# Pairs of heads on the two halves of the array, and bias rows spread in one pass

## Chip, cores and metric
One Trainium2 chip, one core of it. The metric is the device time of one execution in microseconds; three executions of the kernel before gave 1483.94, 1485.22 and 1486.90, median 1485.22.

## What is computed
The input is x of 256 tokens by 1024 features. Two blocks follow each other. The first has two layers under an adaptive norm (shift, scale and gate come from a condition vector): an mLSTM mixer with a SwiGLU FFN, and an HGRN2 mixer with eight experts of which two are taken for each token. The second block is an attention layer with three gated branches and an FFN. What matters here, cut from the reference (256 tokens):

```python
# mLSTM, 8 heads, q and k of 64, v of 128
d = where(mask, b[..., :, None] - b[..., None, :] + li[..., None, :], NEG)   # b = cumsum(log sigmoid f)
m_t = maximum(inter, max(d, axis=-1))                  # a running maximum along the tokens
s = einsum('bhtd,bhsd->bhts', qc, kc) * exp(d - m_t[..., None])
num = ... + einsum('bhts,bhsv->bhtv', s, vc)           # and den = sum of s; h = num / max(|den|, exp(-m_t))

# block attention (moba), 8 heads of 64: with 256 tokens it is causal softmax attention over one block
# forgetting attention (fox), 8 heads of 64
scores = einsum('bhqd,bhkd->bhqk', qc, k) * scale + cq[..., None] - cum[:, :, None, :]
p = softmax(where(causal, scores, -inf));  y = einsum('bhqk,bhkd->bhqd', p, v)
# memory attention, 4 heads of 128, over 256 memory tokens
merged = sigmoid(a_m) * (y_m @ w_br_moba) + sigmoid(a_f) * (y_f @ w_br_fox) + sigmoid(a_c) * (y_c @ w_br_mem)
x = x + merged @ w_out
```

## The kernel before
The activations live transposed, features on the 128 partitions and 256 tokens along the free dimension, in SBUF for the whole program. Weights are streamed from HBM in tiles of 1 MB. Each tile is cut into two fp32r parts: ACT writes the rounded upper part (`whi`, line 175) and VectorE the rest (`wlo`, line 181). A projection is then three fp32r matmuls per chunk (`mm3`: upper by upper, upper by lower, lower by upper). Products between activations, as scores and values, are plain f32 matmuls through `mm` (line 165); in the trace each of these is two passes of weight load and matmul.

PSUM has two sets of four banks of 512 columns: `acc` for the projections and `ps` for all the rest (`bank()`). The framework orders the instructions of each engine at build time, by the order in which the program emits them and by when it reckons their operands to be ready; on the chip each engine takes its list strictly in order. The four banks of a set go round in the order in which the program asks for them. So what the program emits behind a group of head products (for instance the projections for the sigmoid gates, `gates()`, or the next q, `qk()`) is used by that order to fill TensorE between the products of the heads.

*mLSTM.* After the gates, `mrun` [8, 256] holds the running maximum, one row for each head. For each head, one matmul with a column of the identity, repeated over 128 columns, as weights (8 rows, `ident[:8, h]`) spreads that row over all 128 partitions (two f32 passes of 256 columns). Two VectorE operations and an exponential on ACT make the decay matrix. Later a loop over the eight heads takes the scores (q and k of head h lie on partitions 0 to 63 or 64 to 127 of one chunk, so each product uses half of the rows of the array: one matmul of 256 columns, one of 128 for the causal half), multiplies them by the decay, takes the value products on the whole array, and sums over tokens with one-column products into one bank that is held through the loop.

*Causal heads* (`causal_heads`, from line 1265) runs twice, for the block attention without a bias and for the forgetting attention with one. For each of eight heads: a bank, the two score products (64 rows), with a bias two products that spread row h of `cum` [8, 256] (8 rows, four f32 passes), two bf16 products that add the causal mask; then the maximum on VectorE (line 1283), the exponential on ACT, both for two query halves, the reciprocal (1285) and the scaling on VectorE; a bank and three transposes on TensorE (line 1290), a copy to SBUF (line 1292); then the value products, 64 columns of weights, into the upper or lower half of the partitions of a bank that an even head and the odd head behind it share. Behind the odd head `split` makes two fp32r parts of it for the branch's projection. The scores of a head thus wait for a bank that comes free behind an earlier head's transposes or values.

`attention` calls them in the order: q, k and v of moba; the forget logits, their log sigmoid and the running sum `cum`; causal heads of moba; gates; q, k, v of fox; the branch of moba; causal heads of fox; gates; q of the memory heads; the branch of fox; the memory heads.

Of the kernel before, what the change touches and what calls it, by code (L numbers as in the profile page):

```python
# [11 lines left out]
F32 = mybir.dt.float32  # L12
# [126 lines left out]
class Kernel:  # L139
# [61 lines left out]
    def all_weights(self):  # L201
        """the tiles of weights in the order in which the products take them"""
# [39 lines left out]
    def prepare(self, n):  # L242
        """the next n tiles of weights that will be asked for"""
        while len(self.ready) < n and (self.loaded or self.load()):
            self.ready.append(self.parts(self.loaded.popleft()))
# [8 lines left out]
    @contextmanager  # L254
    def behind(self, *instructions):
        """what is ready early stays behind these in the order of issue"""
        with ExitStack() as es:
            for ins in instructions:
                es.enter_context(self.tc.issue_after(ins))
            yield  # L260
# [34 lines left out]
    def last_tile(self, products, ends):  # L295
        """the products of each chunk of 128 columns, chunks of different banks after one another, and
        what comes then, two chunks later for its second part"""
# [15 lines left out]
    def like(self, hl, act, k):  # L313
        """chunk k of what weights, whole or in two parts, are multiplied with"""
        return [x[:, k, :] for x in act] if len(hl) == 2 else (self.full[:, k, :],)

    def proj_t(self, act, n=512, nk=DC, between=None, ends=None):
        """act @ the next n columns of weights, transposed, 256 columns to a bank [P, 2, S]"""
# [26 lines left out]
    def proj_tok(self, act, between=None):  # L345
        """act @ the next 512 columns of weights, tokens on the partitions: one bank for each 128 tokens"""
# [15 lines left out]
    def rsqrt(self, pool, v, tag):  # L362
        """v ** -0.5: a guess from the bits of v, a step of Newton's and one of third order"""
# [19 lines left out]
    def spread(self, out, col, start):  # L383
        """the values col [P, 1] of 128 tokens along the free dimension of every partition"""
        self.mm(out, col.to_broadcast([P, P]), self.cst("ident"), start)

    def token_sums(self, out, sq, start, by=None):
        """out [P, 2, n]: for each token the sums over the partitions of sq [P, S], times by [P, n]"""
# [4 lines left out]
    def stat_begin(self, tag="ps", second=None, together=6):  # L393
        """sums of the squares of x, with second [P, DC, 2] also of x * w, of columns (1, w ** 2)"""
# [7 lines left out]
    def square(self, chunk, c=0):  # L402
        """the squares of chunk c; what is returned sums them over the partitions, the first ones together"""
# [12 lines left out]
    def stat_end(self):  # L416
        """1 / the root mean square of each token on every partition"""
        return self.stat_spread(self.stat_tokens())

    def stat_tokens(self):  # L420
        """1 / the root mean square of each token [P, 2, 1]; with second [P, 2, 2] there is also that
        of the norm of x * w that comes after: with r ** -2 = mean(x ** 2) + EPS it is
        r * (mean((x * w * r) ** 2) + EPS) ** -0.5 = (mean((x * w) ** 2) + EPS * r ** -2) ** -0.5"""
# [8 lines left out]
    def stat_spread(self, r):  # L432
        """[P, 2, n] by token to [P, n, S] on every partition"""
# [10 lines left out]
    def normed(self, x, r, g, shift=None, hold=3):  # L444
        """x * r * g (+ shift) as the pair of parts that the products take"""
# [16 lines left out]
    def scaled(self, x, g, tiles=None):  # L462
        """x * g as the pair of parts that the products take"""
# [8 lines left out]
    def held_factor(self, ps):  # L472
        """a factor for each token, kept on every partition"""
# [4 lines left out]
    def ada_tile(self, layer, j, tag="raw2"):  # L478
        """256 columns of silu(c) @ ada_w + ada_b into two columns of mod"""
# [12 lines left out]
    def ada_until(self, n):  # L492
        """the first n of 48 times 256 columns are done"""
# [10 lines left out]
    def first_norm(self, x):  # L504
        """the norm of x, chunk by chunk as the columns of mod are done; its statistic is under way"""
# [40 lines left out]
    def resid(self, ps, c, gate):  # L546
        """chunk c of x += gate * ps, and its squares for the next norm"""
# [14 lines left out]
    def ffn(self, act, gate=None, between=None, factor=None):  # L562
        """factor gives a factor [P, S] of act that is still to come"""
# [63 lines left out]
    def setup(self):  # L627
# [11 lines left out]
        self.mod = self.t(self.cp, [P, 96], "mod")  # L639

    def conditions(self, pool):
        """silu(c), the same on every partition"""
# [19 lines left out]
    def small(self, out, hl, act):  # L662
        """a product with a few columns of weights, transposed"""
# [3 lines left out]
    def head_norm(self, pool, banks, heads, dst, scale, gain=None, by=None):  # L667
        """banks: 512 columns by token. Each head of a token over its root mean square, times the gain
        [P, head] and turned by the rotary embedding if there is a gain, goes transposed to
        dst [P, 4, S], times scale (a number or [P, 1]). by [P, 2, 1] is a factor of the tokens still to come"""  # L670
# [93 lines left out]
    def memory_norm(self, pool):  # L764
        """the memory times its gain; the factor of each token is still to come"""
# [12 lines left out]
    def log_sigmoid(self, pool, f, tag):  # L778
        """[8, S] rows"""
# [6 lines left out]
        return out  # L786

# [4 lines left out]
    def mlstm(self, pool, act):  # L792
# [47 lines left out]
        decay = []  # L840
        for h in range(8):
            pm = self.bank()
            self.mm(pm[:, :S], self.cst("ident")[:8, h : h + 1].to_broadcast([8, P]), mrun, True)
# [12 lines left out]
        for h in range(8):  # L856
            c, o = h // 2, (h % 2) * 64
            qh, kh = q[o : o + 64, c, :], k[o : o + 64, c, :]
            ps = self.bank()
            self.mm(ps[:, 0:S], kh[:, 0:P], qh, True)  # L860
            self.mm(ps[:, S : S + P], kh[:, P:S], qh[:, P:S], False)
# [21 lines left out]
        # h = num / den, and h over its root mean square is num / sqrt(mean(num ** 2) + EPS * den ** 2)  # L883
# [22 lines left out]
    def lower_bounds(self):  # L906
        """lb and 1 - lb of the second mixer"""
# [8 lines left out]
    def hgrn(self, pool, act):  # L916
# [39 lines left out]
        def scores(q, k, bc, at, cr):  # L956
            """at[s, h, half, t]: the scores inside each half of the tokens, cr across the halves.
            Level n pairs the tokens of each right block of 2^n with the left block beside it; the
            decay is split at the last token of the left block, so no exponent is above 0."""
# [47 lines left out]
        def outputs(g, at, cr):  # L1007
            """the heads' normed outputs"""
# [137 lines left out]
    def experts(self, pool, xt, pos, mask, gate, late):  # L1146
        """the tokens of each expert at slots pos (0 to 127) pass through it, their results are added to x"""
# [117 lines left out]
    def causal_heads(self, pool, q, k, v, y, bias):  # L1265
        """softmax over the keys up to each token; y gets the heads' outputs, transposed"""
        nc = self.nc
        for h in range(8):
            c, o = h // 2, (h % 2) * 64
            qh, kh = q[o : o + 64, c, :], k[o : o + 64, c, :]  # L1270
            ps = self.bank()
            self.mm(ps[:, 0:P], qh[:, 0:P], kh[:, 0:P], True)
            self.mm(ps[:, P:384], qh[:, P:S], kh, False)
            if bias is not None:
                sel = self.cst("ident")[:8, h : h + 1].to_broadcast([8, P])
                self.mm(ps[:, 0:P], sel, bias[:, 0:P], False)
                self.mm(ps[:, P:384], sel, bias, False)
            self.mm(ps[:, 0:P], self.identb, self.upb, False)
            self.mm(ps[:, S:384], self.identb, self.upb, False)
            nm, sm = (self.t(pool, [P, 2], n, 2) for n in ("nm", "sm"))  # L1280
            e = self.t(pool, [P, 384], "e", 2)
            for j, sl in enumerate((slice(0, P), slice(P, 384))):
                nc.vector.tensor_reduce(nm[:, j : j + 1], ps[:, sl], axis=AX.X, op=ALU.max, negate=True)
# [173 lines left out]
```

## Time and profile before
| | us |
|---|---|
| median of three runs | 1485.22 |
| lowest, highest | 1483.94, 1486.90 |
| the profiled execution: span from first to last instruction | 1481.2 |
| TensorE busy | 1429.3 (96%) |
| VectorE busy | 1123.6 (76%) |
| ACT busy | 838.1 (57%) |
| mean granted TensorE clock | 0.977 of full speed |

The page of the profile gives busy time by engine, a picture of the span in slices, the chain of work that ended last and the costliest groups. In rows of a timeline the first column is the start and the second the length of one row (several instructions of one kind behind one another are one row, xN); matmul ends are modelled, so the step from one start to the next is the better measure of what an operation takes. A bracket names the idle time before a row and the engine that ended it. `64*128 64x256` is a weight tile of 64 rows by 128 columns and a moving operand of 64 rows by 256 columns.

### The profile page before, as it was taken

To read this page: it belongs to the slowest core of one execution; us is meant where nothing else is said; L and a number is where in the kernel's file an instruction comes from. 1 tells how busy PE (TensorE), PEld (TensorE's weight loads), DVE (VectorE), ACT (ScalarE), POOL (GpSimd) and SP (SyncE) were. 2 spreads that over 40 slices of the span, in tenths; PEclk is the share of its full clock that TensorE was granted. 3 is DMA by queue.
4 is the path that set the end of the run, shared out by engine and by line. 5 is a ranking of instruction groups with operands and counts; after the bars stand their busy time and mean duration, and the time that the engine had idled before them with its cause. 6 is when DMAs were issued, how large, how long until landed. Compare 5 with 4: busy or idle time off the path is not lost.

```text
span 1481.2 us, 23294 instructions
## 1 busy us (share of the span) xinstructions
PE 1429.3 (96%) x9380; PEld 1292.7 (87%) x9380; DVE 1123.6 (76%) x1738; ACT 838.1 (57%) x1195; POOL 32.9 (2%) x36
## 2 busy tenths in 40 slices
PE   5999899999999998999999999999999999999998
PEld 4789899999999987888888888888878779999998
DVE  6887798887697786897898888888666566765554
ACT  2644444434775655777777777766545355544432
POOL 1000100001000020000000000000000000100000
PEclk7999999999899998999999999999999999999999
DMA  8975599989453334798998998995435234555542
GB/s 335 339 260 195 178 348 353 343 314 337 150 151 109 115 114 145 252 375 309 320 362 305 345 339 303 355 322 192 143 114 169 88 114 143 164 179 191 179 143 86
DMA packets 149508, 343.51 MB, mean 232 GB/s; under 512 B 5904, under 2 KB 27280, under 8 KB 149136
## 3 DMA queue, kind: packets, MB, share of 16 engines
q1 hardware_dynamic: 148240, 341.00, 66.1%
q8 instruction: 76, 1.25, 0.4%
q10 hardware_dynamic: 1152, 0.94, 0.2%
q14 instruction: 40, 0.33, 0.1%
HBM read 340.86 MB, written 1.05 MB: 231 GB/s over the span
## 4 chain that ended last, share of the span: by engine, by line
PE 58%; ACT 1%; DVE 1%; issue 0%; ACTq 0%
PE acc L165 38%; PE ps L165 18%; PE ps L1203 1%; ACT whi L175 1%; PE ps L1290 1%; PE ps L698 0%; DVE wlo L181 0%; ACT L175 0%; PE ps L1413 0%; DVE yel L178 0%; ACT yeh L175 0%; ACT e L175 0%; ACT sg L175 0%; DVE ss L677 0%; DVE e L185 0%
## 5 line engine op out<-in xcount | busy, mean ns | idle before, releaser
L181 DVE TENSOR_TENSOR wlo<-raw,whi 128x1024 fp32r<-128x1024 f32 (+2 forms) x564 | 646.9, 1182 | 148.2 <-ACT whi L175 147.6
L175 ACT ACTIVATE whi<-raw 128x1024 fp32r<-128x1024 f32 (+2 forms) x564 | 547.8, 1016 | 314.1 <-PE acc L165 164.3
L165 PE MATMUL acc<-act_hi,whi 128*128 128x256 f32 x1344 | 382.0, 285 | 2.6 <-ACT act_hi L175 2.4
L165 PE MATMUL acc<-act_lo,whi 128*128 128x256 f32 x1344 | 381.1, 284 | 0.0
L165 PE MATMUL acc<-act_hi,wlo 128*128 128x256 f32 x1344 | 379.6, 283 | 1.3 <-DVE wlo L181 1.3
L165 PEld LDWEIGHTS acc<-act_hi,whi 128*128 128x128 f32 x1344 | 255.2, 190 | 4.7 <-ACT act_hi L175 3.0
L165 PEld LDWEIGHTS acc<-act_hi,wlo 128*128 128x128 f32 x1344 | 255.5, 190 | 1.8 <-DVE wlo L181 1.5
L165 PEld LDWEIGHTS acc<-act_lo,whi 128*128 128x128 f32 x1344 | 255.8, 190 | 0.7
L165 PE MATMUL acc<-whi,act_hi 128*128 128x512 f32 (+1 forms) x560 | 217.5, 388 | 0.1
L165 PE MATMUL acc<-wlo,act_hi 128*128 128x512 f32 (+1 forms) x560 | 216.7, 387 | 0.0
L165 PE MATMUL acc<-whi,act_lo 128*128 128x512 f32 (+1 forms) x560 | 215.6, 385 | 0.0
L165 PEld LDWEIGHTS acc<-whi,act_hi 128*128 128x128 f32 x560 | 105.9, 189 | 20.3 <-issue 0.9
L165 PEld LDWEIGHTS acc<-wlo,act_hi 128*128 128x128 f32 x560 | 105.8, 189 | 20.2 <-issue 1.2
L165 PEld LDWEIGHTS acc<-whi,act_lo 128*128 128x128 f32 x560 | 105.7, 189 | 18.8 <-issue 0.3
L485 DVE SCALAR_TENSOR_TENSOR raw<-raw,cond 128x1024 f32<-128x1024 f32 x96 | 115.3, 1228 | 6.5 <-DMA raw<-in_ada_w_dram 6.5
L165 PE MATMUL ps<-hh,whi 128*128 128x256 f32 x352 | 99.6, 283 | 1.5 <-DVE x L178 1.5
L165 PE MATMUL ps<-hl,whi 128*128 128x256 f32 x352 | 99.5, 283 | 0.0
L165 PE MATMUL ps<-hh,wlo 128*128 128x256 f32 x352 | 99.4, 283 | 0.0
L165 PE MATMUL ps<-wlo,hth 128*128 128x512 f32 x176 | 69.0, 392 | 0.0
L165 PEld LDWEIGHTS ps<-hh,whi 128*128 128x128 f32 x352 | 67.4, 192 | 1.7 <-DVE x L178 1.7
L165 PE MATMUL ps<-whi,htl 128*128 128x512 f32 x176 | 68.8, 391 | 0.0
L165 PE MATMUL ps<-whi,hth 128*128 128x512 f32 x176 | 67.6, 393 | 0.0
(348 smaller groups left out, 1798.2 us busy)
## 6 DMA issues: line engine op xcount, KB each, us to landing
raw<-in_ada_w_dram SPq DMA_DIRECT2D x48, 1024.0 KB, 6.2
raw<-in_moe_w_down_dram SPq DMA_DIRECT2D x40, 1024.0 KB, 6.0
raw<-in_moe_w_up_dram SPq DMA_DIRECT2D x32, 1024.0 KB, 7.3
raw<-in_moe_w_gate_dram SPq DMA_DIRECT2D x32, 1024.0 KB, 7.1
raw<-in_w_in_dram SPq DMA_DIRECT2D x26, 1024.0 KB, 5.2
raw<-in_h_w_in_dram SPq DMA_DIRECT2D x16, 1024.0 KB, 5.8
raw<-in_m_w_in_dram SPq DMA_DIRECT2D x12, 1024.0 KB, 7.3
raw<-in_moe_w_gate_dram SPq DMA_DIRECT2D x16, 768.0 KB, 5.5
```

The source lines that it names most:

```text
L165: self.nc.tensor.matmul(out, l, r, start=start, stop=True, skip_group_check=True)
L175: return self.nc.scalar.activation(out, in_, f, **k)
L181: return self.nc.vector.tensor_tensor(out, a, b, op=op)
L485: last = self.nc.vector.scalar_tensor_tensor(w[:, i, :], in0=w[:, i, :], scalar=1.0, in1=self.cond, op0=ALU.mult, op1=ALU.mult, accum_out= ...
L1203: nc.tensor.transpose(hps[:, f * P : (f + 1) * P], h[:, f * P : (f + 1) * P], self.cst("ident"))
L1290: nc.tensor.transpose(pt[:, j * P : (j + 1) * P], e[:, j * P : (j + 1) * P], self.cst("ident"))
```

## The change
Three things are altered; in the rest of the diff comments and docstrings go.

1. Rows are spread by a product of 128 rows. `two_rows` makes a zeroed [128, 256] fp32r tile with the rounded rows in partitions 0 to 7 and what the rounding left in partitions 32 to 39. `row` multiplies it in one fp32r pass by a column of `pick`, which has ones at h and at 32 + h. `mrun` and `cum` both go this way; the tile of `cum` is made before the causal heads of moba.
2. In the mLSTM the score products of heads h and h + 1 are emitted together for even h, into two banks, in turn on rows 0 to 63 and 64 to 127.
3. `causal_heads` loops over four pairs: the score products of both heads in turn, the bias rows of both, the masks of both; the softmax, transposes and copy of each; then one bank and the value products of both in turn on the two column halves, and `split`. The buffers for e, p, the maxima and sums stay two each.

```diff
+        self.pick = self.t(self.cp, [P, 8], "pick", 1, F32R)
+        nc.vector.tensor_tensor(self.pick, self.cst("ident")[:, 0:8], self.cst("ident")[:, 32:40], op=ALU.add)
...
+    def two_rows(self, pool, rows, tag):
+        both = self.t(pool, [P, S], tag, 1, F32R)
+        self.nc.gpsimd.memset(both.bitcast(F32), 0.0)
+        self.act(both[0:8, :], rows, AF.Copy)
+        self.tt(both[32:40, :], rows, both[0:8, :].bitcast(F32), ALU.subtract)
+        return both
+
+    def row(self, out, both, h, start):
+        self.mm(out, self.pick[:, h : h + 1].to_broadcast([P, P]), both, start)
...
+        mrows = self.two_rows(pool, mrun, "mrows")
         for h in range(8):
             pm = self.bank()
-            self.mm(pm[:, :S], self.cst("ident")[:8, h : h + 1].to_broadcast([8, P]), mrun, True)
+            self.row(pm[:, :S], mrows, h, True)
...
         for h in range(8):
-            c, o = h // 2, (h % 2) * 64
-            qh, kh = q[o : o + 64, c, :], k[o : o + 64, c, :]
-            ps = self.bank()
-            self.mm(ps[:, 0:S], kh[:, 0:P], qh, True)
-            self.mm(ps[:, S : S + P], kh[:, P:S], qh[:, P:S], False)
+            c = h // 2
+            if h % 2 == 0:
+                pair = [self.bank() for _ in range(2)]
+                halves = [(ps, q[o : o + 64, c, :], k[o : o + 64, c, :]) for ps, o in zip(pair, (0, 64))]
+                for ps, qh, kh in halves:
+                    self.mm(ps[:, 0:S], kh[:, 0:P], qh, True)
+                for ps, qh, kh in halves:
+                    self.mm(ps[:, S : S + P], kh[:, P:S], qh[:, P:S], False)
+            ps = pair[h % 2]
...
+        queries = (slice(0, P), slice(P, 384))
+        for c in range(4):
+            pair = [(self.bank(), q[o : o + 64, c, :], k[o : o + 64, c, :]) for o in (0, 64)]
+            for ps, qh, kh in pair:
+                self.mm(ps[:, 0:P], qh[:, 0:P], kh[:, 0:P], True)
+            for ps, qh, kh in pair:
+                self.mm(ps[:, P:384], qh[:, P:S], kh, False)
             if bias is not None:
...
+                for i, (ps, qh, kh) in enumerate(pair):
+                    self.row(ps[:, 0:P], bias[:, 0:P], 2 * c + i, False)
+                    self.row(ps[:, P:384], bias, 2 * c + i, False)
+            for ps, qh, kh in pair:
+                self.mm(ps[:, 0:P], self.identb, self.upb, False)
+                self.mm(ps[:, S:384], self.identb, self.upb, False)
+            probs = []
+            for ps, qh, kh in pair:
...
+                probs.append(p)
+            po = self.bank()
+            heads = [(po[i * 64 : i * 64 + 64], v[:, :, (2 * c + i) * 64 : (2 * c + i + 1) * 64], p) for i, p in enumerate(probs)]
+            for out, vh, p in heads:
+                self.mm(out[:, :S], vh[:, 0, :], p[:, :S], True)
+            for out, vh, p in heads:
+                self.mm(out[:, P:S], vh[:, 1, :], p[:, S:384], False)
+            self.split(y[0][:, c, :], y[1][:, c, :], po[:, :S])
...
+            cum = self.two_rows(pool, cum, "cumrows")
             sa = gates(self.causal_heads(pool, q, k, v, y, None))
```

## Rows read from the trace of the kernel before

**Rows 1.** The page: busy time of each engine, and the chain that ended last.
```profile
PE 1429.3 (96%) x9380; PEld 1292.7 (87%) x9380; DVE 1123.6 (76%) x1738; ACT 838.1 (57%) x1195; POOL 32.9 (2%) x36
...
PE 58%; ACT 1%; DVE 1%; issue 0%; ACTq 0%
```

**Rows 2.** Stretches, mLSTM rows: us, busy of each engine, PE clock, DMA share, GB/s.
```profile
62.00:71.80 9.80, 9.62 (x38) 5.73 (x36) 9.01 (x25) 6.63 (x11) 0.00 (x0) 1.00 0.96 347
71.80:78.60 6.80, 6.80 (x15) 4.51 (x15) 5.32 (x12) 4.66 (x8) 0.00 (x0) 0.50 0.42 135
```

**Rows 3.** Stretches, causal heads of moba and of fox, same columns.
```profile
1054.00:1112.00 58.00, 56.79 (x342) 44.39 (x342) 38.84 (x89) 28.69 (x59) 0.00 (x0) 1.00 0.34 112
...
1140.00:1206.00 66.00, 63.37 (x395) 49.72 (x394) 37.31 (x83) 27.04 (x55) 0.00 (x0) 0.99 0.33 108
```

**Rows 4.** Timeline of TensorE, one fox head and the next: start, us, operation.
```profile
1140.03 0.92 PE L165 MATMUL ps<-k,q 64*128 64x128 f32 x4
1140.88 0.92 PE L165 MATMUL ps<-cum,cst_base 8*128 8x128 f32 x4
1141.73 0.29 PE L165 MATMUL ps<-upb,identb 128*128 128x128 bf16 x2
...
1147.35 0.28 PE L165 MATMUL acc<-act_lo,whi 128*128 128x256 f32 x1
1147.47 0.28 PE L165 MATMUL acc<-act_hi,wlo 128*128 128x256 f32 x1
1147.68 0.86 PE L165 MATMUL ps<-p,raw 128*64 128x256 f32 x4
1148.48 0.92 PE L165 MATMUL ps<-k,q 64*128 64x128 f32 x4
```

**Rows 5.** Timeline of TensorE, mLSTM heads.
```profile
100.53 0.81 PE L165 MATMUL ps<-p,v 128*128 128x256 f32 x4
101.18 0.73 PE L165 MATMUL ps<-cst_base,p 128*128 128x1 f32 x6
101.84 0.70 PE L165 MATMUL ps<-q,k 64*128 64x256 f32 x2
102.46 0.61 PE L165 MATMUL ps<-cst_base,sq 128*128 128x1 f32 x4
103.00 0.49 PE L165 MATMUL ps<-q,k 64*128 64x128 f32 x2
103.41 0.38 PE L165 MATMUL acc<-act_hi,whi 128*128 128x256 f32 x1
```

**Rows 6.** Timeline of TensorE, fp32r passes of 128 columns.
```profile
692.05 0.64 PE L165 MATMUL ps<-identr,disp 128*128 128x128 f32 x4
692.53 0.34 PE L165 MATMUL ps<-disp,xth 128*128 128x256 f32 x1
```

**Rows 7.** Timeline of TensorE, rows of mrun: three heads together, one alone.
```profile
64.31 1.56 PE L165 MATMUL ps<-mrun,cst_base 8*128 8x256 f32 x6
65.70 0.23 PE L837 MATMUL ps<-cst_base,floor 8*128 8x8 f32 x2
...
67.23 0.69 PE L165 MATMUL ps<-mrun,cst_base 8*128 8x256 f32 x2
67.85 0.50 PE L165 MATMUL acc<-whi,act_lo 128*128 128x512 f32 x1
```

**Rows 8.** Timeline of TensorE, the last fox head: masks, transposes.
```profile
1198.40 0.29 PE L165 MATMUL ps<-upb,identb 128*128 128x128 bf16 x2
...
1203.48 0.61 PE L1290 MATMUL ps<-cst_base,e 128*128 128x128 f32 x3 [1.65 <-DVE e L185]
```

**Rows 9.** Stretch behind the last fox head, columns as in rows 2.
```profile
1205.00:1208.40 3.40, 2.93 (x13) 2.32 (x12) 2.65 (x7) 2.06 (x5) 0.00 (x0) 0.50 0.00 0
```

**Rows 10.** Operations on tile mrun: duration ns min/median/max, starts, shapes.
```profile
L181 DVE TENSOR_TENSOR floor<-bsum,mrun x1: 401/401/401, 64.5 to 64.5; 8x256 f32<-8x256 f32 x1
```

**Rows 11.** Timeline of TensorE, first moba head's transpose.
```profile
1062.63 0.30 PE L1290 MATMUL ps<-cst_base,e 128*128 128x128 f32 x1 [1.01 <-DVE e L185]
```

More of the change, by code (lines that the diff above doesn't have):

```diff
@@ L1267, in causal_heads @@
         nc = self.nc
[L1268 to L1273, printed above, removed]
-            if bias is not None:
[L1275 to L1283, printed above, removed]
-                last = self.act(e[:, sl], ps[:, sl], AF.Exp, bias=nm[:, j : j + 1], accum_out=sm[:, j : j + 1])
-            nc.vector.reciprocal(sm, sm)
-            for j, sl in enumerate((slice(0, P), slice(P, 384))):
-                self.ts(e[:, sl], e[:, sl], sm[:, j : j + 1], ALU.mult)
-            pt = self.bank()
-            for j in range(3):
-                nc.tensor.transpose(pt[:, j * P : (j + 1) * P], e[:, j * P : (j + 1) * P], self.cst("ident"))
-            p = self.t(pool, [P, 384], "p", 2)
-            nc.vector.tensor_copy(p, pt[:, :384])
-            if h % 2 == 0:
-                po = self.bank()
-            vh = v[:, :, h * 64 : (h + 1) * 64]
-            self.mm(po[o : o + 64, :S], vh[:, 0, :], p[:, :S], True)
-            self.mm(po[o : o + 64, P:S], vh[:, 1, :], p[:, S:384], False)
-            if h % 2:
-                self.split(y[0][:, c, :], y[1][:, c, :], po[:, :S])
@@ new lines, in causal_heads @@
+        queries = (slice(0, P), slice(P, 384))
[5 more added lines that the diff above has]
+                self.mm(ps[:, P:384], qh[:, P:S], kh, False)
+            if bias is not None:
+                for i, (ps, qh, kh) in enumerate(pair):
[6 more added lines that the diff above has]
+            for ps, qh, kh in pair:
+                nm, sm = (self.t(pool, [P, 2], n, 2) for n in ("nm", "sm"))
+                e = self.t(pool, [P, 384], "e", 2)
+                for j, sl in enumerate(queries):
+                    nc.vector.tensor_reduce(nm[:, j : j + 1], ps[:, sl], axis=AX.X, op=ALU.max, negate=True)
+                    last = self.act(e[:, sl], ps[:, sl], AF.Exp, bias=nm[:, j : j + 1], accum_out=sm[:, j : j + 1])
+                nc.vector.reciprocal(sm, sm)
+                for j, sl in enumerate(queries):
+                    self.ts(e[:, sl], e[:, sl], sm[:, j : j + 1], ALU.mult)
+                pt = self.bank()
+                for j in range(3):
+                    nc.tensor.transpose(pt[:, j * P : (j + 1) * P], e[:, j * P : (j + 1) * P], self.cst("ident"))
+                p = self.t(pool, [P, 384], "p", 2)
+                nc.vector.tensor_copy(p, pt[:, :384])
+                probs.append(p)
[6 more added lines that the diff above has]
+            self.split(y[0][:, c, :], y[1][:, c, :], po[:, :S])
```

## The prediction

> **What bounds the kernel now.** I read the page's busy shares and its chain of waits first. TensorE is busy 96% of the span, and nearly all of the chain that the page gives to an engine is TensorE, with ACT and VectorE at 1% each [rows 1]. So a microsecond of TensorE time taken away should come off the end, and a microsecond in which TensorE stands, in its order, behind an operand goes on. Next I looked at the table of stretches for the stages that the diff touches. In the mLSTM's rows stage (62 to 71.8) TensorE is busy 9.62 of 9.80 us and VectorE 9.01; the stage behind it runs at a granted clock of 0.50, the lower level of 1.2 GHz, for 6.8 us [rows 2]. In the two stages of causal heads TensorE is busy 56.79 of 58 and 63.37 of 66 us, VectorE 38.84 and 37.31, ACT less [rows 3]. Last I read the timeline of TensorE, where the distance from one row's start to the next is what an operation costs in the queue; the durations themselves overlap.
>
> **The sum, part by part.** It is made against the profiled execution: span 1481.2 us. The median of the runs is 1485.2, so 4.0 us lie around the span, and I keep them.
>
> (a) *Bias rows of the Fox heads.* Before, each head has four f32 passes with 8 rows of weights, 0.85 us from start to start (1140.88 to 1141.73) [rows 4]. After, it has two fp32r passes, one of 128 and one of 256 columns. The first size costs 0.12 (four from 692.05 to 692.53) [rows 6], the second 0.12 too (1147.35 to 1147.47) [rows 4]; together 0.24, and I take 0.26. Eight heads: 8 x (0.85 - 0.26) = **-4.7**. Bounds: 0.24 to 0.48 a head, -4.9 to -3.0.
>
> (b) *Fewer switches between whole and half array.* A score group (4 passes, 768 columns) takes 0.85 and a value group 0.80 (1147.68 to 1148.48), with 0.09 more for entering (0.21 instead of 0.12 in front of it, 1147.47 to 1147.68) [rows 4]. Four passes of the same columns on all 128 rows, without a switch, take 0.65 (100.53 to 101.18) [rows 5]. A pair of heads therefore costs 2 x 0.85 + 2 x 0.80 + about 3 x 0.09 = 3.57 us where streaming alone is 2.60; 0.97 is switching, in four places. After the change there are two such places in a pair, so half goes: 0.485 x 8 pairs = **-3.9**. Bounds: -2 (if the groups' own fill is in the 0.97) to -5.
>
> (c) *The two halves at once.* No row of before has products of different halves behind one another, so this is bounded from both sides. Nothing: the passes follow each other as now. All: passes of 0.108 (128 columns) and 0.217 (256), which is 0.65 over 768 columns [rows 5], in the new order A,A,B,B | A,A,B,B, where only neighbours of different halves overlap: 0.108 + 0.108 + 0.217 + 0.217 + 0.217 = 0.87 instead of 1.30. That saves 0.43 in each of 16 groups (scores and values of 8 pairs), 6.9 us. I take **-5.0**, nearer to the upper end: consecutive passes already overlap in the array in these rows (0.28 long at 0.12 spacing) [rows 4], so the engine does not finish one before it starts the next. A loss I exclude: the same passes with the same columns are issued. The Trainium skill, page TensorEngine Tiling (Array Packing), section Key Properties, says that different tiles can load weights and multiply in parallel, and that a change of the tiling mode drains the engine. The second half agrees with the 0.85 against 0.65; the first no row here shows. By the page alone (c) would be -6.9 and (d) 0.8 more, and the time 1460.1, an estimate from that page.
>
> (d) *mLSTM scores.* A head's two products cost 0.62 (101.84 to 102.46) and 0.41 (103.00 to 103.41) with about 0.10 for entering: 1.13 [rows 5], 2.26 a pair. Two groups at 0.65 and one entry and exit (0.28) are 1.58. Four pairs: -2.7. At once would give up to 4 x 0.43 = 1.7 more; I take half, 0.9, because the token sums hold one of the four banks and the second head's scores must wait for a bank to come free. **-3.6**, bounds -2 to -4.4. TensorE has whole-array products of gates and values beside it (100 us and after).
>
> (e) *mLSTM rows.* Three heads behind one another take 1.39 (64.31 to 65.70), a lone one 0.62 (67.23 to 67.85) [rows 7]: 1.39 + 5 x 0.62 = 4.5; after, 8 x 0.12 = 1.0. **-3.5**, bounds -2.5 (VectorE, 92% busy there, is late with the decay) to -4.6 (the entries go too).
>
> (f) *The half-clock stretch behind them.* 6.8 us at 0.50 cost 3.4 us over full clock [rows 2]. What the engine did before it fell was the alternation of 8-row passes with whole ones; the half-clock stretch of [rows 9] follows waits and no such rows, so I take half: **-1.7**, bounds 0 and -3.4.
>
> (g) *The end of the Fox stage.* TensorE is not busy for 2.63 us of the stage [rows 3], mostly in front of the last head's transposes (1.65 us on VectorE) [rows 8], and then runs 3.4 us at half clock, busy 2.93 of them [rows 9], so another 1.5. The cause is eight softmaxes in series: one takes 5.0 us from the masks (1198.40) to the first transpose (1203.48) [rows 8], the scores of a head come only after the values of the one before. Pairs put two chains beside each other, so that the four pairs end sooner than TensorE's work. **-3.0**, bounds 0 and -4.1.
>
> (h) *Costs.* The two parts of the rows are an ACT copy and a VectorE subtraction on 8 x 256, about 0.4 us each (the row nearest to it is 401 ns) [rows 10], and a POOL clearing. Those of Fox are made ahead of the causal heads of the first branch, 80 us before use: nothing. Those of the mLSTM delay its rows by 0.8, behind projections that TensorE has anyway, with more than 15 us until the first decay is used: nothing, and 0.8 without that cover. The selector is one small VectorE operation at the start: nothing. The new order makes new waits: the next pair's scores need banks that come free with the transposes and values of this one, and behind transposes in TensorE's order stand projections that need nothing. One such wait of 1.01 us stands in the first branch before (1062.63) [rows 11]. I take three of them, at the first and last pairs: **+3.0**, bounds 0 and 8.
>
> Sum: -4.7 - 3.9 - 5.0 - 3.6 - 3.5 - 1.7 - 3.0 + 3.0 = **-22.4**. Span 1458.8, time 1462.8: I say **1463**.
>
> **Rivals.** *Halves not at once.* The two halves share what streams; then (c) and the 0.9 of (d) are gone: -16.5, time **1468.7**. For it: no row shows such overlap, and f32 passes come in twos of the same half. Against: the overlap of neighbours in the array.
>
> *The saved time in the attention becomes waiting.* Then scores, masks and values are quick but the softmaxes, on VectorE and ACT, are the length of a stage; (a), (b), (c), (g) are lost, 16.6: -5.8, time **1479.4**. For it: the waits at 1203 and 1062. Against: VectorE is busy only 37.31 of 66 us [rows 3], and two chains beside each other have more slack than one. The Trainium skill, same page, section PSUM Bottleneck, has this as a rule: tiling speeds up TensorE but not what empties PSUM. The busy shares here do not bear it out for a whole stage.
>
> *Slower: TensorE stands at every pair.* The projections that fill a softmax are put in TensorE's order at build time. If they are spent ahead of the first pairs, TensorE stands for most of one chain, say 3.5 of the 5.0 us [rows 8], at each of 8 pairs: 28 us instead of the 3.0 of (h), and (g) isn't saved: -22.4 + 25 + 3.0 = +5.6, time **1490.8**. It decides from 2.8 us a pair on. For it: after the change both heads' values of a pair wait for both softmaxes, and no scores of another pair stand between. Against: the fill of a stage, 63.4 busy less 8 heads of about 3.0 (0.85 + 0.85 + 0.80 and masks, transposes and entries) or some 39 us, is about as long as four chains of pairs.
>
> *The change doesn't do what it says*, for example the scheduler takes the products of a pair apart again: then (a) and (e) alone remain, -8.2, time 1477.0.
>
> **How the numbers follow.** Forecast 0.45, halves not at once 0.30, waiting 0.12, slower 0.08, taken apart 0.05. The forecast's own range, with the bounds of (c), (f), (g) and (h), is 1453 to 1468. Ranges of the first rival, 1465 to 1473, and some of the waiting case put the range that should hold 8 in 10 at **1453 to 1480**. About 0.2%, 3 us, is what a measurement can tell from no change: faster takes the forecast, the first rival, most of the waiting case and the last, 0.85; same some of the waiting case and of the slower one, 0.07; slower 0.08.
>
> **What would show it.** Fox scores of a pair at about 0.9 to 1.1 us from the first product to the first row product is (c); 1.3 or more is the first rival. Rows of a head at 0.25 is (a). The stretch at about 72 at a clock of 1.00 is (f); the Fox stage without idle time in front of the last transposes is (g). If TensorE's idle time in front of transposes and values in the two stages sums to more than 8 us, (h) is wrong, and above 22 the kernel is slower. The prediction is wrong if the granted clock falls in the new pair groups, or if a stretch outside these stages moves by more than 2 us.

## The result, and the profile after

| | before | after |
|---|---|---|
| median, first measurement (4 runs each) | 1484.58 | 1466.79 (1455.06 to 1472.68) |
| median, second measurement (15 and 6 runs) | 1484.13 | 1466.96 (1462.43 to 1471.64) |
| ratio, with its 95% interval | | 0.9873 [0.9842, 0.9903], then 0.9881 [0.9859, 0.9903] |
| profiled execution: span, mean granted clock | 1481.2, 0.977 | 1470.9, 0.969 |

The kernel is 17 to 18 us faster; 22 were forecast, and the time lies inside the stated range. Single runs of one kernel differ by up to 18 us here, so from now on a term is read from a trace wherever a trace can show it, and the times, by median and ratio, are the check on it.

**The pairs.** The timeline of TensorE in the changed kernel, a Fox pair's scores, rows and masks (start, length, operation):

```profile
1143.90 0.28 PE L165 MATMUL acc<-yh,wlo 128*128 128x256 f32 x1
1144.11 0.93 PE L165 MATMUL ps<-k,q 64*128 64x128 f32 x8
1144.96 0.72 PE L165 MATMUL ps<-cumrows,pick 128*128 128x128 f32 x4
1145.53 0.40 PE L165 MATMUL ps<-upb,identb 128*128 128x128 bf16 x4
...
1152.04 1.22 PE L165 MATMUL ps<-p,raw 128*64 128x256 f32 x8
1153.20 0.93 PE L165 MATMUL ps<-k,q 64*128 64x128 f32 x8
```

Eight score passes, two heads, go in 0.85 us (1144.11 to 1144.96), as long as four took for one head [rows 4]; in the single records the passes of the two halves start 7 ns apart. The rows of both heads take 0.57 instead of 2 x 0.85. The values of both take 1.16 instead of 2 x 0.80: they too run side by side, but the second head's start 0.36 later, right when its copy of p ends. VectorE's timeline of the same kernel shows the two copies in one row, so that the second ends at 1152.35; the second head's first pass starts at 1152.40:

```profile
1151.22 1.13 DVE L1315 COPY p<-ps 128x384 f32<-128x384 f32 x2 [0.48 <-PE ps L1313]
```

**The waits.** Of TensorE's timeline in the changed kernel, three places at which it stands (the last column is the idle time and what ended it):

```profile
66.21 0.29 PE L851 MATMUL ps<-cst_base,floor 8*128 8x8 f32 x2 [0.81 <-ACT floor L175]
66.43 0.61 PE L165 MATMUL ps<-mrows,pick 128*128 128x256 f32 x3
66.88 0.40 PE L165 MATMUL acc<-whi,act_lo 128*128 128x512 f32 x1
...
76.69 0.47 PE L165 MATMUL acc<-whi,act_hi 128*128 128x512 f32 x1 [1.70 <-DVE conv L178]
...
1067.88 0.30 PE L1313 MATMUL ps<-cst_base,e 128*128 128x128 f32 x1 [2.08 <-DVE e L185]
```

The first two are new. The third answers to [rows 11] and is twice as long. The end of the Fox stage has none of the idle time of [rows 8]; the longest step from the start of one matmul to the next in that stage is 0.65 us, at 1167.5.

**The clock.** Stretches of the changed kernel (us, busy of PE, PEld, DVE, ACT, POOL, then the granted clock): the two that answer to [rows 2], and the loop over the mLSTM's heads.

```profile
62.00:71.80 9.80, 8.80 (x43) 6.96 (x43) 8.91 (x26) 6.40 (x11) 0.00 (x0) 1.00 0.92 345
71.80:78.60 6.80, 5.10 (x26) 3.82 (x26) 5.83 (x11) 6.77 (x13) 0.00 (x0) 1.00 0.20 74
95.00:135.00 40.00, 40.00 (x208) 36.56 (x207) 19.37 (x39) 11.12 (x22) 0.00 (x0) 0.66 0.47 167
```

and the same loop in the kernel before:

```profile
95.00:135.00 40.00, 40.00 (x290) 36.51 (x290) 25.81 (x50) 13.94 (x25) 0.00 (x0) 1.00 0.74 259
```

The half-clock stretch at 72 is gone. But the loop, which ran at the full 2.4 GHz before, now spends 27 of its 40 us at 1.2 GHz (clock 0.66), though TensorE is busy for all of it. In the 40 us it does 208 matmuls instead of 290. That was in no term of the forecast.

### The profile page after: what moved, and what is told of

It is laid out like the page before. It is cut to its first block, busy times and chain, and to the rows that moved or that the text cites. A ratio compares the mean times of both kernels' runs of the same rounds, so it can differ in the third digit from the quotient of the medians.

```text
span 1470.9 us, 23270 instructions
## 1 busy us (share of the span) xinstructions
PE 1416.9 (96%) x9356; PEld 1293.3 (88%) x9356; DVE 1122.9 (76%) x1741; ACT 837.9 (57%) x1197; POOL 33.8 (2%) x38
## 4 chain that ended last, share of the span: by engine, by line
PE 57%; ACT 1%; DVE 1%; issue 0%; ACTq 0%
PE acc L165 38%; PE ps L165 17%; PE ps L1222 1%; ACT whi L175 0%; PE ps L1313 0%; DVE wlo L181 0%; PE ps L700 0%; ACT e L175 0%; ACT L175 0%; PE ps L1438 0%; DVE yel L178 0%; ACT yeh L175 0%; ACT sg L175 0%; DVE ss L679 0%; DVE nm L1306 0%
## 5 line engine op out<-in xcount | busy, mean ns | idle before, releaser
L165 PE MATMUL acc<-act_lo,whi 128*128 128x256 f32 x1344 | 385.0, 287 | 0.0
L165 PEld LDWEIGHTS acc<-act_hi,whi 128*128 128x128 f32 x1344 | 258.6, 193 | 4.7 <-ACT act_hi L175 3.0
L165 PEld LDWEIGHTS acc<-act_hi,wlo 128*128 128x128 f32 x1344 | 258.9, 193 | 1.6 <-DVE wlo L181 1.5
L165 PEld LDWEIGHTS acc<-act_lo,whi 128*128 128x128 f32 x1344 | 259.0, 193 | 1.1 <-issue 0.4
```

What stands on the lines that cost most here:

```text
L165: self.nc.tensor.matmul(out, l, r, start=start, stop=True, skip_group_check=True)
```

## The experiments

Twelve kernels, in three lots; kernels of a lot ran on the same chip. The kernel before, run beside each lot, gave 1484.13, 1485.07 and 1485.91, so between lots the ratios to it compare better than the medians. The first lot asked for the parts, the second for the mLSTM's loss, the third for its cause and the single terms.

**again.** The changed kernel as it is.

> The changed kernel once more, to see which half-clock stretches of its first profile come back. Theory A (the drops of the granted clock at 102 to 133 us, 27 us at half, are chance): they are absent or elsewhere, span some 1457 to 1462, median near 1467. Theory B (the pairs in the mLSTM's score loop bring them about): they stand at the same place, span near 1471.

1466.96 us; the loop fell again (clock 0.74 between 95 and 135 us, 20 us at half), at 108 and 118 instead of 102 and 120. Theory A is out and B stands, by the place and by the span (1469.9); the median is that of the first measurement.

```profile
95.00:135.00 40.00, 40.00 (x235) 37.15 (x235) 21.28 (x44) 12.36 (x23) 0.00 (x0) 0.74 0.49 174
```

**rows_only.** Heads one by one, as before; rows by `two_rows` and `row` (here against the kernel before; the mLSTM's rows as in the change).

```diff
-                sel = self.cst("ident")[:8, h : h + 1].to_broadcast([8, P])
-                self.mm(ps[:, 0:P], sel, bias[:, 0:P], False)
-                self.mm(ps[:, P:384], sel, bias, False)
+                self.row(ps[:, 0:P], bias[:, 0:P], h, False)
+                self.row(ps[:, P:384], bias, h, False)
```

> Only the bias rows are spread in one pass (mLSTM and Fox), heads are taken one by one as before. Theory A (what is saved is time in TensorE's queue): Fox rows -4.5, mLSTM rows -4, new waits in the mLSTM's rows stage +1 to +3: 1477 to 1481 beside 1484.6 of before. Rival (the saving is that two softmaxes go beside each other, rows are worth nothing): 1484.

1471.90 us, ratio 0.9914 [0.9894, 0.9934]: 12.2 us faster than before, more than either theory said. My expectation had left out two terms of the forecast, (f) and (g). The loop is at full clock, in place of the stretch at 72 stands one of 3.4 us from 77.5, and the last Fox head's transposes no longer wait. TensorE's timeline at that head (the masks, then the first transpose, with no idle time in front):

```profile
1189.53 0.28 PE L165 MATMUL ps<-upb,identb 128*128 128x128 bf16 x2
...
1194.46 0.30 PE L1304 MATMUL ps<-cst_base,e 128*128 128x128 f32 x1
```

The softmax takes as long as in [rows 8], but each head now takes less of TensorE, so projections are left to fill the last one. The pairs were not needed for that.

**mlstm_scores_alone.** The changed kernel with the mLSTM's two score products head by head.

```diff
-            if h % 2 == 0:
-                pair = [self.bank() for _ in range(2)]
...
-            ps = pair[h % 2]
+            ps = self.bank()
+            self.mm(ps[:, 0:S], kh[:, 0:P], qh, True)
+            self.mm(ps[:, S : S + P], kh[:, P:S], qh[:, P:S], False)
```

> The changed kernel with the mLSTM's score products head by head as before; rows and causal heads stay changed. If the pairs save queue time there and the clock is chance: 3 to 4 us above the changed kernel, 1470. If the pairs bring about the half-clock stretches at 102 to 133 us: those are gone and it is up to 10 us below, 1457 to 1463.

1463.14 us (1459.13 to 1463.98), ratio 0.9852 [0.9830, 0.9875]: 3.8 us below the changed kernel. The two intervals overlap, so the times alone would not settle it; the clock does, 1.00 in the loop:

```profile
95.00:135.00 40.00, 39.97 (x291) 36.57 (x290) 25.83 (x52) 14.87 (x27) 0.00 (x0) 1.00 0.65 230
```

**scores_apart.** The changed kernel; in the causal heads the first head's scores, rows and masks stand ahead of the second's.

```diff
-            for ps, qh, kh in pair:
-                self.mm(ps[:, 0:P], qh[:, 0:P], kh[:, 0:P], True)
-            for ps, qh, kh in pair:
-                self.mm(ps[:, P:384], qh[:, P:S], kh, False)
...
+            for i, (ps, qh, kh) in enumerate(pair):
+                self.mm(ps[:, 0:P], qh[:, 0:P], kh[:, 0:P], True)
+                self.mm(ps[:, P:384], qh[:, P:S], kh, False)
+                if bias is not None:
+                    self.row(ps[:, 0:P], bias[:, 0:P], 2 * c + i, False)
+                    self.row(ps[:, P:384], bias, 2 * c + i, False)
+                self.mm(ps[:, 0:P], self.identb, self.upb, False)
```

> The changed kernel, but in the causal heads the first head's scores, rows and masks all come before the second head's, so a whole-array product stands between the halves; banks, softmaxes and values stay in pairs. Theory A (the halves run at once, 0.85 us for both heads' scores instead of 2 x 0.85): 8 pairs x 0.85 to 1.1 = 7 to 9 us above the changed kernel, 1474 to 1476. Rival (the gain is the order of the softmaxes in pairs): as the changed kernel, 1467.

1472.20 us, ratio 0.9924 [0.9897, 0.9951]: 5.2 us above the changed kernel by median, 6.4 by ratio. Theory A, a little under its size. TensorE's timeline:

```profile
1137.56 0.92 PE L165 MATMUL ps<-k,q 64*128 64x128 f32 x4
1138.41 0.49 PE L165 MATMUL ps<-cumrows,pick 128*128 128x128 f32 x2
1138.74 0.28 PE L165 MATMUL ps<-upb,identb 128*128 128x128 bf16 x2
1138.96 0.92 PE L165 MATMUL ps<-k,q 64*128 64x128 f32 x4
```

A head alone takes 1.40 us (1137.56 to 1138.96), so a pair 2.8, where the changed kernel has 1.62 (1144.11 to 1145.73). The loop of the mLSTM, which still has its pairs, fell here too (0.87), so in the times some clock is mixed in.

**no_sums.** The changed kernel without the mLSTM's token sums.

```diff
+        self.mm(sums, self.cst("ident"), self.cst("ones")[:, 0:1].to_broadcast([P, 32]), True)
...
-            self.token_sums(sums[:, 0, :, h : h + 1], p[:, :S], h == 0)
-            self.mm(sums[:, 0, 1, h : h + 1], p[:, S:384], self.cst("ones")[:, 0:1], False)
...
-            self.token_sums(sums[:, 1, :, h : h + 1], sq, False)
```

> The changed kernel with the token sums of the mLSTM's heads left out (the one-column products with p and with the squares; the bank is filled once with ones). They take some 9 us of TensorE's queue. Theory C (the clock falls in the pairs' loop because the one-column products of two heads now stand close together): no half-clock stretch between 95 and 135 us, so 9 + 10 us off: near 1448. Rival (two half arrays at once, or the pairs as such, bring the clock down): stretches of 10 to 27 us at half stay, only the 9 us go: near 1458.

1451.14 us, 15.8 below the changed kernel (15.3 by ratio), and the loop is at full clock although its pairs are there, and whole, in all four places:

```profile
95.00:135.00 40.00, 39.41 (x286) 37.14 (x286) 34.98 (x70) 19.44 (x33) 0.00 (x0) 1.00 0.77 276
```

So two half arrays at once do not by themselves bring the clock down. (The pairs of the causal heads say the same: 1.00 between 1144 and 1179 us in the changed kernel. Its moba stage has one half-clock stretch, 3.4 us from 1068.4; it follows the wait that ends at 1067.88.)

**one_pn.** The changed kernel with the value products of a pair in one bank.

```diff
-            pn = self.bank()
+            if h % 2 == 0:
+                both = self.bank()
+            pn = both[:, h % 2 * S : (h % 2 + 1) * S]
```

> The changed kernel, but the value products of both mLSTM heads of a pair go into one bank, so a pair needs three banks beside the one of the sums, and its two score products need not wait apart. If the loss in the mLSTM is the waiting for banks that tears pairs apart: 3 to 5 us below the changed kernel, 1462 to 1464. If it is the clock and has to do with pairs as such: half-clock stretches of 10 us and more stay between 95 and 135 us, and the time is within 2 us of the changed kernel, 1467.

1475.83 us, 8.9 above the changed kernel (7.9 by ratio), which neither theory said. The clock in the loop is the lowest of all:

```profile
95.00:135.00 40.00, 40.00 (x183) 34.44 (x181) 16.44 (x29) 8.40 (x18) 0.00 (x0) 0.61 0.47 171
```

The edit did not keep the pairs whole: in the trace the 256-column passes of the two heads stand apart, at 98.34 and 100.17, with one-column products between them, and only the 128-column passes are together (102.90). So what the waiting for banks costs is not tested by this kernel. What it adds is another order of the same products in which the clock falls: TensorE goes through products of both heads from 97.03 to 103.63 before the next projection, and the fall, at 100.1, comes inside that group.

**alone_act_copy.** Scores of the mLSTM head by head, and ACT copies the second head's p.

```diff
-                nc.vector.tensor_copy(p, pt[:, :384])
+                if probs:
+                    self.act(p, pt[:, :384], AF.Copy)
+                else:
+                    nc.vector.tensor_copy(p, pt[:, :384])
```

> The kernel with mLSTM scores head by head (1463.1), and in the causal heads ACT instead of VectorE copies the second head's transposed p. Theory: the second head's value products start 0.36 us after the first head's because its p comes 0.47 us later off VectorE; with two engines they start in step, value groups of a pair take 0.80 to 0.95 instead of 1.17: 2 to 3 us off, 1460 to 1461. Rival (the column halves can't start together): groups stay at 1.1 to 1.2, same time.

1460.16 us, ratio 0.9827 [0.9807, 0.9846]. It has the lowest median of the kernels that leave nothing out, 3.0 below the one without the copy on ACT (3.7 by ratio), but the two intervals overlap. In the traces it takes 116.0 us from the first score product of moba to the last value product of Fox, against 118.3, and 1.7 of that is a half-clock stretch which only the other profile has there; that leaves 0.6. TensorE's timeline has the expected group in one place of the eight; three others are torn, and four stay between 1.1 and 1.3 us. In these the second head's last transpose starts 0.57 us behind the first's (1142.16 and 1142.73 in the Fox pair whose values start at 1143.29), whichever engine copies. The one place:

```profile
1081.42 0.87 PE L165 MATMUL ps<-p,raw 128*64 128x256 f32 x8
1082.22 0.93 PE L165 MATMUL ps<-k,q 64*128 64x128 f32 x8
```

0.80 us (1081.42 to 1082.22) for both heads, as long as one: so the column halves can run together, and the rival's reason is out. The gain in time stays open.

**alone_floor_first.** Scores head by head, and the two parts of the mLSTM's rows behind floor's exponential.

```diff
-        mrows = self.two_rows(pool, mrun, "mrows")
+        with self.behind(fexp.ins):
+            mrows = self.two_rows(pool, mrun, "mrows")
```

> The kernel with mLSTM scores head by head (1463.1), with the two parts of the mLSTM's rows made behind the exponential of floor on ACT. Theory: the ACT copy of the rows, put ahead of the table load, made floor 0.8 us late, and TensorE stood 1.1 us for it at 65 us; that wait goes: 1 us off, 1462. Rival: the rows come later and the wait for the convolution behind them (1.9 us) grows by as much: same time.

1463.84 us, the rival: the wait at 65 us is gone, but from the last score product at 74.22 to the next projection 2.8 us pass instead of 2.0, and the half-clock stretch that begins there lasts 6.8 us instead of 3.4.

**alone_double_sums.** Scores head by head; each token sum is taken twice, so the sums are doubled.

> The kernel with mLSTM scores head by head (1463.1), with each token sum of the mLSTM taken twice, which doubles the sums. Ten one-column products more for each head, with two passes each: some 9 us of TensorE's queue at full clock, with the projections between the heads as they were. Theory C (the clock falls when one-column products and switches fill too much of the loop, with or without pairs): half-clock stretches appear between 95 and 140 us, and the time is 9 + 5 to 15 us more, 1477 to 1487. Rival (only the pairs' order brings them): full clock in the loop, 1472.

1488.02 us, 24.9 above the kernel with scores alone (23.3 by ratio), 9 of which were expected for the products themselves. (They are five products more for each head, ten passes: x12 and x8 below instead of x6 and x4.) No pair is there, and the clock falls, 41 us at half in the loop and behind it:

```profile
95.00:135.00 40.00, 40.00 (x213) 36.58 (x211) 15.16 (x25) 7.64 (x14) 0.00 (x0) 0.68 0.47 170
```

This is Theory C's side. TensorE's timeline just ahead of the first fall, at 102.2:

```profile
98.52 0.82 PE L165 MATMUL ps<-p,v 128*128 128x256 f32 x4
99.17 1.40 PE L165 MATMUL ps<-cst_base,p 128*128 128x1 f32 x12
100.50 0.70 PE L165 MATMUL ps<-q,k 64*128 64x256 f32 x2
101.12 1.05 PE L165 MATMUL ps<-cst_base,sq 128*128 128x1 f32 x8
102.11 0.70 PE L165 MATMUL ps<-q,k 64*128 64x128 f32 x2
102.74 0.58 PE L165 MATMUL acc<-act_lo,whi 128*128 128x256 f32 x1
```

and the same in the changed kernel, whose clock fell at 102.4:

```profile
96.64 0.82 PE L165 MATMUL ps<-p,v 128*128 128x256 f32 x4
97.29 0.73 PE L165 MATMUL ps<-cst_base,p 128*128 128x1 f32 x6
97.88 0.68 PE L165 MATMUL ps<-p,v 128*128 128x256 f32 x2
98.39 0.50 PE L165 MATMUL ps<-cst_base,sq 128*128 128x1 f32 x4
98.76 0.47 PE L165 MATMUL ps<-p,v 128*128 128x128 f32 x2
99.06 0.73 PE L165 MATMUL ps<-cst_base,p 128*128 128x1 f32 x6
99.72 0.70 PE L165 MATMUL ps<-q,k 64*128 64x256 f32 x2
100.35 0.61 PE L165 MATMUL ps<-cst_base,sq 128*128 128x1 f32 x4
100.88 0.92 PE L165 MATMUL ps<-q,k 64*128 64x256 f32 x6
101.73 0.39 PE L165 MATMUL acc<-act_lo,whi 128*128 128x256 f32 x1
```

In the changed kernel 5.1 us (96.64 to 101.73) of values, one-column products and half-array scores of two heads stand without a projection between them, with doubled sums 4.2 us (98.52 to 102.74) of one head; before, a head's 2.9 us [rows 5] were followed by projections. So pairs with the sums bring the clock down, and so do doubled sums without pairs; with either the pairs or the sums taken away the loop is at full clock. The clocks of all runs bear the profiles out in the main: over the whole span the mean is 0.969 to 0.980 in the ten runs of the changed kernel, 0.978 to 0.983 in five with scores alone, 0.984 to 0.985 in four without sums and 0.966 to 0.975 in ten with doubled sums.

**alone_not_in_turn.** Scores of the mLSTM head by head; in the causal heads both score products of the first head are issued ahead of both of the second.

```diff
             for ps, qh, kh in pair:
                 self.mm(ps[:, 0:P], qh[:, 0:P], kh[:, 0:P], True)
-            for ps, qh, kh in pair:
                 self.mm(ps[:, P:384], qh[:, P:S], kh, False)
```

> The kernel with mLSTM scores head by head (1463.1); in the causal heads both score products of the first head are issued ahead of both of the second, not in turn. Theory D (each half has a queue of its own and the engine hands out several passes ahead): the passes run side by side as before, 0.85 to 1.0 us a pair, same time within 2 us. Rival (only neighbours in the order overlap): 1.3 us and more a pair, 3 to 4 us more, 1467.

1460.75 us, ratio 0.9849 [0.9830, 0.9867]: the same. Taking them in turn is not what makes them run together; the group still takes 0.86:

```profile
1051.38 0.93 PE L165 MATMUL ps<-k,q 64*128 64x128 f32 x8
1052.24 0.40 PE L165 MATMUL ps<-upb,identb 128*128 128x128 bf16 x4
```

**mlstm_before.** The changed kernel with the mLSTM wholly as before: its rows and its scores as in the minus lines of the diff.

> The changed kernel with the whole mLSTM as before (rows by 8-row f32 products, scores head by head); causal heads changed. Against the kernel with mLSTM scores head by head (1463.1) this undoes the mLSTM rows alone. Forecast steps (e) and (f) with the stretch gone for good: 4 + 3.4 = 7 us more, 1470, and the granted clock falls near 72 us. Rival (the fall at 72 us was chance): 3 to 4 us more, 1467.

1466.16 us, ratio 0.9882 [0.9862, 0.9903], so the rows of the mLSTM are worth 3.0 us by median and 4.4 by ratio beside the kernel with scores alone. From their traces it is 3.5, by the start of the FFN's first product with hh (221.94 and 218.46). The stretch at 72 is back, nearly at its old place and of its old length:

```profile
71.80:78.60 6.80, 6.80 (x16) 4.46 (x16) 5.32 (x14) 5.23 (x10) 0.00 (x0) 0.57 0.47 152
```

So it comes and goes with the 8-row products, as (f) had supposed, and the rival's reason fails. The size is the rival's: without these products there are the new waits at 66 and 76 us, and the other trace has a half-clock stretch of 3.4 us from 77.5.

**alone_fox_rows_before.** Scores of the mLSTM head by head, the Fox rows as before.

```diff
-                    self.row(ps[:, 0:P], bias[:, 0:P], 2 * c + i, False)
-                    self.row(ps[:, P:384], bias, 2 * c + i, False)
+                    sel = self.cst("ident")[:8, 2 * c + i : 2 * c + i + 1].to_broadcast([8, P])
+                    self.mm(ps[:, 0:P], sel, bias[:, 0:P], False)
+                    self.mm(ps[:, P:384], sel, bias, False)
```

> The kernel with mLSTM scores head by head (1463.1), with the Fox rows by 8-row f32 products as before. Step (a) of the forecast: 0.85 instead of 0.28 us a head, 4.5 to 5 us more, 1468. Rival (the time is hidden behind the softmaxes): same.

1466.47 us, ratio 0.9877 [0.9858, 0.9895]: 3.3 to 3.7 us more. Not hidden; a little under the 4.5 that the trace gives.

## Why the prediction was nearly right

Three kernels cut the way into steps: before 1484.1, with rows alone 1471.9, with pairs in the causal heads 1463.1, with pairs in the mLSTM 1467.0. The forecast for these steps was -12.9 [(a), (e), (f), (g)], -5.9 [(b), (c), (h)] and -3.6 [(d)]; they measured -12.2, -8.8 and +3.8. That the total is only 5 us off is in part luck: the causal heads gave 2.9 more than forecast, and (d) came out 7.4 worse. By the time alone the rival "halves not at once" (1468.7) is nearer to the measured 1466.8 than the forecast (1463) is; what decides against it is the 0.85 us of the trace. The forecast's own range, 1453 to 1468, is also not what its bounds add up to: those of (c), (f), (g) and (h) give 1455 to 1477.

- (a) -4.7: 4 x (2 x 0.85 - 0.57) = -4.5 in the trace, -3.3 to -3.7 by runs. Right.
- (b) and (c) -8.9: the scores of a pair went from 2 x 0.85 and an entry to 0.85, the values from 2 x 0.80 to 1.16. The halves run in step, not only neighbour beside neighbour as I had chained them (0.87 plus switching). What I had read as overlap, lengths of 0.28 at steps of 0.12, is no evidence for it, since the ends of matmuls are modelled; the starts 7 ns apart are. In step the bound is 16 x 0.65 = 10.4 us, not the 6.9 that I had taken. What that gave beyond the estimate was taken back by the later second p and where the order tears a pair apart (five of the eight value groups of the changed kernel). The Trainium skill, page TensorEngine Tiling (Array Packing), section Key Properties, says that different tiles can load weights and multiply in parallel. The trace agrees: 0.85 us for eight score passes and 0.80 for eight value passes. The rival "halves not at once" is out.
- (d) -3.6, **the step that failed**. Its queue time was sized well; what failed is that the clock had no term. The FFN's first product with hh starts at 226.63 in the changed kernel and at 218.46 with scores alone. The start, and the stretches from 31 us to there, first in the changed kernel, then with scores alone:

```profile
226.63 0.28 PE L165 MATMUL ps<-hh,whi 128*128 128x256 f32 x1
31.00:95.00 64.00, 60.16 (x324) 49.52 (x323) 58.34 (x114) 42.01 (x63) 0.00 (x0) 1.00 0.82 303
135.00:226.60 91.60, 86.34 (x673) 84.91 (x672) 76.68 (x140) 40.64 (x57) 6.06 (x5) 0.94 0.70 253
...
218.46 0.28 PE L165 MATMUL ps<-hh,whi 128*128 128x256 f32 x1
31.00:95.00 64.00, 59.59 (x302) 48.58 (x301) 58.32 (x116) 40.73 (x61) 0.00 (x0) 0.97 0.82 303
135.00:218.50 83.50, 78.11 (x609) 76.71 (x610) 71.19 (x127) 38.24 (x54) 6.10 (x5) 0.94 0.68 249
```

  The half clock cost the one 40.0 x 0.34 + 91.6 x 0.06 = 19.1 us and the other 64.0 x 0.03 + 83.5 x 0.06 = 6.9 us. Without that it is 207.5 against 211.6, so the pairs save 4.1. But they cost 12.2 more in clock. This cost differs from one execution to the next: the second profile of the changed kernel gives 10.8 (17.7 lost, product at 225.29), and scores_apart, whose mLSTM is the same, only 3.3 (10.2 lost, product at 217.95), with the same saving of about 4. The medians, 3.8 us slower for 4 us of saving, put it at some 8 in an ordinary run, an estimate. That the granted clock falls in the new pair groups was named as what would make the prediction wrong, and had no term.
- (e) and (f) -5.2: the rows went from 5.1 us (the last two heads at half clock) and their entries to 1.0 (steps from start to start, summed over the eight heads), and the half-clock stretch at 72 went with them. Not all of (f) is kept: in seven of the twelve profiles with the new rows a half-clock stretch begins between 76.4 and 78.3, behind the wait for the convolution, 3.4 us long (6.8 in alone_floor_first). Both terms were right, and both were paid for in part by two new waits of 1.2 and 2.0 us (start to start), at floor and at the convolution. (h) had placed its 3 us in the causal heads; there it was 1.1 (the first transpose of moba, 2.36 instead of 1.29 from the product before), and 3.4 us at half clock behind it in the first profile. In the mLSTM's rows I had held the cover to be enough: the ACT copy of the rows went ahead of the table load that floor needs, as the order of ACT shows:

```profile
64.01 0.42 ACT L175 ACTIVATE mrows<-mrun 8x256 fp32r<-8x256 f32 x1 [1.99 <-DVE mod L181]
64.45 1.28 ACT L175 ACT_TABLE_LOAD   x1
65.74 0.41 ACT L175 ACTIVATE floor<-floor 8x256 f32<-8x256 f32 x1
```

  In the kernel before the load came ahead, at 62.19, and floor's exponential at 64.94.
- (g) -3.0: the idle time and the half clock at the end of the Fox stage went, but for another reason than the one given. Rows alone did it; two softmaxes beside each other were not needed.
- The rivals "waiting" and "slower": of TensorE's steps in the causal heads' stages only two exceed 0.6 us, 2.36 and 0.65, far from waits of 2.8 a pair.
- The other sign of being wrong, a stretch outside these stages that moves by more than 2 us, did not show between that product with hh and the first score product of moba: 833.2 us before (220.79 to 1054.03), 833.8 after (226.63 to 1060.46).

What stays open is whether it is the one-column products or the switches between them and the other products that bring the clock down, and why it falls by so much more in one execution than in another. A kernel with all pairs and sums, but with projections put between the two heads, was not run. Also open is whether the copy on ACT gains anything.

The version to take from here is the changed kernel with the mLSTM's scores head by head: 1463.1, 0.9852 of before, and 1460.2 (0.9827) with the copy on ACT.

## What to carry to other kernels

Here two f32 products of 64 rows, or of 64 columns, on different halves of the array took no longer than one where both operands were there (0.85 and 0.80 us a group); what held a pair up was the later operand, not the order of issue. And a regrouping that saved 4 us of queue time cost 3 to 12 us in granted clock, in a stage in which TensorE never stood idle; with projections between the heads' small products, as with scores alone, the clock stayed up. So beside each sum of queue times a look at the granted clock of the stage belongs, and a mention of what the regrouping brings together.

## What was not expected of the hardware

- Eight f32 passes of two heads run as four steps, not chained as neighbours: 7 ns between the two halves when issued in turn and 13 ns when one head's passes are issued ahead of the other's. In the value group at 1152.04 the first head's 128-column passes start at 1152.52 and 1152.63, between the second head's two 256-column ones (1152.40 and 1152.67). No list of whole products has these starts in its order, so "strictly in order", as the kernel is described above, does not hold between the two halves.
- The clock fell with TensorE busy 40.00 of 40 us: to a mean of 0.66, 0.74, 0.87 and 0.61 between 95 and 135 us in the four profiles of kernels with mLSTM pairs and sums, 0.68 with doubled sums and no pairs, and 1.00 in the nine others. The Trainium skill, page TensorE: Matmul & The Clock Gate, section HAM oscillation, tells of the clock falling through idle gaps of the engine. In these five profiles the trace shows no idle time in the loop, so the measurement adds a case to it.
- The first 20 us at half clock, from 10 to 31 us, are in some executions and not in others of the same kernel (the changed kernel has them in the first profile and not in the second), and the span hardly differs (1470.9 and 1469.9). In that stage TensorE isn't the bound: it is busy 9.65 and 9.38 of the 21 us from 10 to 31.
